# Two groups of matmuls on constants in the first stage of a transformer block

## The chip, the cores and the metric

The kernel runs on one core of a Trainium2 chip. The metric is device time in microseconds of one execution. The core has five engines with queues of their own: PE (TensorE, matrix products and transpositions into the PSUM banks), DVE (VectorE), ACT (ScalarE), POOL (GpSimd) and SP (SyncE, which here issues the DMA transfers). Each works through its instructions in order, and an instruction waits until what it needs from another engine is done.

## The reference

One layer of a trunk with 1024 positions and width 1024, in f32: a token mixer (a short gated convolution beside a stick-breaking attention with 8 heads of 64) and a squared-ReLU MLP. The first stage of the kernel computes the beginning of it: the modulation of the conditioning vector `c`, the normalised and modulated `h`, and the attention's values `v`.

```python
mod = c @ w_ada[l] + b_ada[l]
sh1, sc1, gt1, sh2, sc2, gt2 = jnp.split(mod, N_MOD, axis=-1)

h = modulate(rms_norm(x, g_pre_mix[l]), sh1, sc1)   # h * (1 + sc1) + sh1
proj = h @ w_in[l]
bg, cg, u, q, k, v, ga, gb = jnp.split(proj, split_pts, axis=-1)
y_conv = short_conv_branch(bg, cg, u, conv_w[l]) @ w_proj_conv[l]
o = stick_breaking_attention(q, k, v)               # heads split and joined
merged = jax.nn.sigmoid(ga) * y_conv + jax.nn.sigmoid(gb) * (o @ w_proj_attn[l])
x = x + gt1[:, None, :] * rms_norm(merged @ w_out[l], g_post_mix[l])

h2 = modulate(rms_norm(x, g_pre_mlp[l]), sh2, sc2)
ff = jnp.square(jax.nn.relu(h2 @ w_mlp_in[l])) @ w_mlp_out[l]
x = x + gt2[:, None, :] * rms_norm(ff, g_post_mlp[l])
```

## The kernel before

Products of f32 data are made of three products of split operands: a tensor is split into a rounded part (`hi`, an ACT copy at L104) and the rest (`lo`, a DVE subtraction at L91), and hi x hi, hi x lo and lo x hi are summed in PSUM. The kernel runs through the first stage (modulation, `h` and values), attention with the projections and the convolution, the branches, `w_out`, and the MLP, whose products use a scheme with seven products in place of eight.

The change is in the first stage alone. There positions go in blocks `b` of 128 (0 to 7) and channels in columns `k` of 128 (0 to 7). The stage is written as steps, each a letter and its numbers; a string `order` lists them, and `run` (L524) calls them in turn. `tc.manual_schedule` at L535 keeps the queues of PE and SP in that written order. The orders of ACT, DVE and POOL come from the compiler's planner, which goes by modelled times.

The steps, with the lines at which the profile shows them:

- `x` (`x_block`): loads a block of `x` and normalises it (ACT L403 and L407, or DVE L409; the root on POOL, L132).
- `T` (`turn_all`): transposes all eight columns of a block on PE (L418) into banks with the tag `tr`, of which there are two, and copies them to `xT` (L422). It is used for the blocks 0 to 3.
- `s` (`slab`): loads two columns of `w_ada` for the shift and the scale in four pieces (L440) and sums them, weighted by `c`, on DVE into `acc` (L449 for the first piece, L451 for the others).
- `g` (`gains`): sums `acc` over the partitions with four PE matmuls of one column each (L461). They write four columns of the bank `mod`, which the profile calls `c`. DVE reads two pairs of these columns (L94, into a1 and b1) and finishes a1 (L464). Shifts of `mod` use the columns 0 to 7, scales 8 to 15.
- `w` (`value_rows`): loads rows of `w_in` for the values (L470) and splits them (L104, L91).
- `t` (`turn`): transposes column `k` of one or three blocks into a `tr` bank (L483). Group letters: A is the blocks 0 to 3, B is block 4, C is 5 to 7; a, d, b and c are 0 to 1, 2 to 3, 4, and 5 to 7.
- `h` (`shift`): makes `h` of a column from `xT` or from a `tr` bank, times a1 plus b1, and splits it: ACT L494 with DVE L495, or ACT L498 and L104, then DVE L91 (`hTl`).
- `v` (`values`): three matmuls of 512 columns for each block and column (L508) into one bank per block.

So g02 is the sums of the first slab (columns 0 and 1), va0 the values of blocks 0 and 1 from column 0, tB6 the transposition of column 6 of block 4. The PE queue near the first place holds, in this order, g02, va0, vd0, tB1, tB0, vd1, tB4, vb0, tB2, g22, vb1, va1, tB3; then tB6, vb2, va2, g42, vd2, va3, vb3, vd3, va4, vd4, g62, and after vd5 further on tB5. Each `tr` bank is free again when `shift` has read it.

`ident` and `ones` are constants of 128 x 128 f32 that POOL writes at the start. `mod` is one bank of 512 f32 columns, in use through this stage only.

Of the kernel before, what the change touches and what calls it, by code (L numbers as in the profile page):

```python
# [16 lines left out]
P = 128  # L17
D = 1024
T = 1024
# [7 lines left out]
HALF = 512  # L27
# [3 lines left out]
def block_kernel(  # L31
# [19 lines left out]
    nc = tc.nc  # L51
    x, out = x[0], out[0]
# [28 lines left out]
    def bank(pool, tag, bufs=None):  # L81
        return pool.tile([P, HALF], F32, tag=tag, name=nm(tag), bufs=bufs)
# [267 lines left out]
    ident = cst.tile([P, P], F32, name="ident")  # L350
    make_identity(nc, ident)
    ones = cst.tile([P, P], F32, name="ones")
# [21 lines left out]
    with ExitStack() as es:  # L374
# [15 lines left out]
        mod = bank(pst, "c", 1)  # L390
# [94 lines left out]
        def shift(k, blocks):  # L485
# [6 lines left out]
            hi, lo = hT[0][:, k, to], hT[1][:, k, to]  # L492
            if (k, blocks[0]) in BOTH:
                nc.scalar.activation(hi, src, AF.Identity, scale=ak, bias=bk)  # L494
# [6 lines left out]
        def values(k, blocks):  # L501
            for b in blocks:
# [9 lines left out]
                if k == KC - 1:  # L512
# [2 lines left out]
                        vs[:, b, :, 0, :], vs[:, b, :, 1, :],  # L515
                    )

        BOTH = {(7, 4), (4, 0), (0, 4), (1, 5), (0, 0), (5, 4), (6, 4), (0, 5), (6, 0), (1, 0)}
        NORM_ACT = {2, 3, 4, 7}
        TURN_DVE = {(1, 0), (1, 1), (2, 1)}  # L520
        groups = {"A": (0, 1, 2, 3), "B": (4,), "C": (5, 6, 7), "a": (0, 1), "d": (2, 3), "b": (4,), "c": (5, 6, 7)}
        steps = {"x": x_block, "T": turn_all, "s": slab, "g": gains, "w": value_rows}

        def run(order):  # L524
            for step in order.split():
# [4 lines left out]
                    {"t": turn, "h": shift, "v": values}[what[0]](*n, groups[what[1]])  # L530

        order = """
            x1 x0 x2 T1 x3 s02 T0 T3 T2 g02 hA0 w02 va0 x4 s22 hA1 vd0 tB1 tB0 hB0 w22 vd1 tB4 vb0 hB1 tB2 g22 hB2 vb1 hA2 va1 s42 hA3 tB3 tB6 vb2 va2 hB3 g42 vd2 w42 hA5 va3 vb3 hA4 vd3 s62 x5 va4 hB4 x6 vd4 g62 tB7 vd5 w62 hA6 vb4 va5 x7 hB6 tB5 vd6 va6 hA7 hB5 hB7 vb5 tC0 hC0 tC5 va7 hC5 vb6 tC1 hC1 tC2 vd7 tC3 vc0 hC2 tC4 hC3 tC6 vc1 vc2 tC7 vc3 hC4 vc4 hC6 hC7 vc5 vc6 vb7 vc7
        """
        with tc.manual_schedule(engines={mybir.EngineType.PE, mybir.EngineType.SP}):  # L535
            run(order)
# [723 lines left out]
    steps = [(g, i) for g in range(NG) for i in ORDER]  # L1260
# [236 lines left out]
```

## Time and profile before

| what | us |
|---|---|
| median of three runs | 1435.9 |
| lowest and highest of them | 1434.11, 1441.1 |
| the profiled execution, whole | 1439.44 |
| its span | 1437.7 |

| stretch, us from the start | PE busy | DVE busy | ACT busy | granted clock |
|---|---|---|---|---|
| 0 to 20 | 9.06 | 9.62 | 11.42 | 1.00 |
| 20 to 40 | 12.12 | 18.41 | 11.99 | 0.80 |
| 40 to 60 | 18.66 | 17.36 | 13.55 | 0.94 |
| 60 to 260 | 190.03 | 140.59 | 113.26 | 0.98 |

The first table is device time; the span is the part of the profiled execution in which the engines work. In the second, busy times are sums over the stretch, and the granted clock is PE's, as a share of full speed, averaged over it.

A row of a timeline gives the start, the duration (of several instructions together where a count stands behind), the engine, the line, the operation, output and inputs by name, their shapes, and in brackets how long the engine stood idle before and what ended that. A row of a view of stretches gives the stretch, its length, the busy time of PE, PE's weight loads, DVE, ACT and POOL with their numbers of instructions, the granted clock, the busy share of the DMA engines and GB/s. A row of the view of waits names who waited for whom, the total, how often, and the longest.

### The profile page before, as it was taken

Reading aid. Unit: us, or ns where it says so; the run is one execution under the profiler, and the core shown is the slowest. Engines: PE = TensorE matmul, PEld = TensorE weight load, DVE = VectorE, ACT = ScalarE, POOL = GpSimd, SP = SyncE. Lnnn points to the kernel's source line nnn. Section 1 sums busy time; section 2 is a strip of 40 time slices with the busy share of each in tenths; the row PEclk is TensorE's granted clock in tenths of the full one; section 3 lists DMA queues with packets and bytes.
Section 4 is the critical chain, followed back from the end, with each engine's and each line's share of the span. In section 5 each row is a group of like instructions: output and inputs, shape, how many; then the busy total and the mean of one; then the engine's idle time right before and its main releaser. Section 6 shows DMA issues by size and latency. Waiting matters only on the chain.

```text
span 1437.7 us, 17905 instructions
## 1 busy us (share of the span) xinstructions
PE 1368.7 (95%) x6281; PEld 1120.3 (78%) x6281; DVE 1058.7 (74%) x1656; ACT 653.7 (45%) x1317; POOL 97.2 (7%) x187
## 2 busy tenths in 40 slices
PE   5899899999999999989999899999999999999996
PEld 4788777887888888767878688888888788888884
DVE  6827888887876878637736886555654999898987
ACT  5736656565524444324446634333332554343343
POOL 1003112212200000000001000000000000000002
PEclk9999999999999999999999999999999999999998
DMA  8601110111124776668422243322346452514113
GB/s 296 187 15 39 32 53 22 37 38 52 45 90 141 249 269 199 208 203 319 149 97 100 68 146 117 117 82 95 117 144 221 160 169 83 176 59 154 49 47 117
DMA packets 111741, 178.42 MB, mean 124 GB/s; under 512 B 7786, under 2 KB 67230, under 8 KB 111652
## 3 DMA queue, kind: packets, MB, share of 16 engines
q1 hardware_dynamic: 111652, 177.29, 37.3%
q8 instruction: 49, 0.80, 0.2%
q14 instruction: 40, 0.33, 0.1%
HBM read 135.83 MB, written 41.43 MB: 123 GB/s over the span
## 4 chain that ended last, share of the span: by engine, by line
PE 71%; DVE 14%; DMA 6%; issue 4%; ACT 3%; POOL 1%; SPq 0%; DVEq 0%; ACTq 0%; POOLq 0%
PE s L234 26%; PE s L1371 18%; PE mm L546 10%; PE s L903 3%; PE v L508 3%; DVE pt L690 2%; PE s L122 2%; PE s L123 2%; PE s L121 2%; PE o L731 2%; DMA raw<-in_w_in_dram 2%; DVE a L694 2%; DMA wa<-in_w_ada_dram 2%; PE tr L720 1%; POOL a L686 1%
## 5 line engine op out<-in xcount | busy, mean ns | idle before, releaser
L1371 PE MATMUL s<-y,y 128*128 128x512 f32 x1008 | 239.6, 390 | 0.0
L1371 PEld LDWEIGHTS s<-y,y 128*128 128x128 f32 x1008 | 189.3, 188 | 40.4
L546 PE MATMUL mm<-hTh,wh 128*128 128x512 f32 x320 | 129.1, 403 | 0.0
L546 PE MATMUL mm<-hTh,wl 128*128 128x512 f32 x320 | 125.6, 392 | 0.0
L546 PE MATMUL mm<-hTl,wh 128*128 128x512 f32 x320 | 125.5, 392 | 0.0
L104 ACT CAST y<-g 128x512 fp32r<-128x512 f32 x96 | 53.5, 620 | 114.7 <-PE s L1371 97.0
L690 DVE TENSOR_TENSOR_SCAN pt<-pt,dmask 128x128 f32<-128x128 f32 (+3 forms) x64 | 87.1, 1365 | 8.6 <-ACT pt L683 8.2
L234 PE MATMUL s<-mTh,g 128*128 128x512 f32 x256 | 86.0, 403 | 3.7 <-ACT mTh L104 3.7
L1371 PE MATMUL s<-fr,fr 128*128 128x512 f32 x336 | 87.1, 392 | 1.5 <-DVE fr L91 1.5
L104 ACT CAST tu<-tr 128x512 fp32r<-128x512 f32 (+2 forms) x112 | 49.2, 439 | 78.2 <-PE tr L720 51.6
L132 POOL TENSOR_TENSOR rstd<-var,mhalf 128x1 f32<-128x1 f32 x32 | 25.2, 789 | 871.5 <-DVE var L129 871.4
L91 DVE TENSOR_TENSOR tu<-tr,tu 128x512 fp32r<-128x512 f32 (+2 forms) x112 | 55.1, 494 | 34.5 <-ACT tu L104 33.4
L234 PE MATMUL s<-mTh,h 128*128 128x512 f32 x240 | 79.6, 395 | 0.0
L1381 DVE TENSOR_TENSOR ffacc<-s,ffacc 128x512 f32<-128x512 f32 x96 | 65.5, 691 | 16.9 <-PE s L1371 16.9
L1371 PEld LDWEIGHTS s<-fr,fr 128*128 128x128 f32 x336 | 63.0, 188 | 16.0 <-DVE fr L91 1.9
L234 PE MATMUL s<-y,h 128*128 128x512 f32 x288 | 71.7, 391 | 0.0
L234 PE MATMUL s<-y,g 128*128 128x512 f32 x288 | 71.5, 391 | 0.0
L546 PEld LDWEIGHTS mm<-hTh,wl 128*128 128x128 f32 x320 | 60.2, 188 | 13.4
L234 PE MATMUL s<-hTh,t 128*128 128x512 f32 x208 | 67.6, 394 | 0.0
L546 PEld LDWEIGHTS mm<-hTl,wh 128*128 128x128 f32 x320 | 60.5, 189 | 8.8
L546 PEld LDWEIGHTS mm<-hTh,wh 128*128 128x128 f32 x320 | 60.4, 189 | 8.9
L731 PE MATMUL o<-tu,vs 128*128 128x256 f32 x320 | 56.9, 297 | 9.7 <-DVE ot L741 5.1
(286 smaller groups left out, 3124.0 us busy)
## 6 DMA issues: line engine op xcount, KB each, us to landing
raw<-in_w_in_dram SPq DMA_DIRECT2D x38, 512.0 KB, 5.2
wa<-in_w_ada_dram SPq DMA_DIRECT2D x32, 512.0 KB, 4.0
raw<-in_w_mlp_in_dram SPq DMA_DIRECT2D x32, 512.0 KB, 3.8
f_d<-wl SPq DMA_DIRECT2D x16, 512.0 KB, 4.8
f_d<-wh SPq DMA_DIRECT2D x16, 512.0 KB, 3.2
g<-in_w_mlp_out_dram SPq DMA_DIRECT2D x32, 256.0 KB, 3.7
g<-f_d SPq DMA_DIRECT2D x32, 256.0 KB, 3.2
h<-in_w_mlp_out_dram SPq DMA_DIRECT2D x32, 256.0 KB
```

The costliest lines, as they stand in the source:

```text
L91: eng.tensor_tensor(o, a, b, op=ALU.subtract)
L104: nc.scalar.copy(hi, src)
L121: nc.tensor.matmul(ps, lh, rh, start=i == 0, stop=False)
L122: nc.tensor.matmul(ps, lh, rl, start=False, stop=False)
L234: nc.tensor.matmul(ps, l, r, start=first and k == 0 and j == 0, stop=k == nk - 1 and j == 2, skip_group_check=True,)
L508: nc.tensor.matmul(vb[b], l, r, start=k == 0 and i == 0, stop=k == KC - 1 and i == 2, skip_group_check=True,)
L546: nc.tensor.matmul(ps, w[a][:, k, :], hT[b][:, k, s], start=k == 0 and i == 0, stop=k == KC - 1 and i == 2, skip_group_check=True,)
L690: nc.vector.tensor_tensor_scan(pt[:, 0:w][:, ::-1], pt[:, 0:w][:, ::-1], dmask[:, T - w : T][:, ::-1], 1.0, ALU.mult, ALU.max,)
L731: nc.tensor.matmul(po[:, : 2 * P], v, part[:, 0:5:4, :] if j and jp == g else part[:, 2 * j + 1 : 2 * j + 3, :], start=jp == 0 and j == 0 ...
L903: nc.tensor.matmul(ps, l[:, k, s], r, start=k == 0 and i == 0, stop=k == 3 and i == 2, skip_group_check=True,)
L1371: nc.tensor.matmul(ps, l[:, s], r, start=start and j == 0 and n == 0, stop=stop and j == len(fs) - 1 and n == 2, skip_group_check=True,)
L1381: nc.vector.tensor_tensor(o, ps, o, op=ALU.add)
```

## The change

A step `z` is new. It issues `n` matmuls whose operands are the constants: `ones` is the weights, `ident` the 128 moving columns, both f32. The output goes to the last 128 columns of the bank `mod` (384 to 511), and nothing reads it. The step z8 stands in the order twice: behind g02 (ahead of hA0, so ahead of va0 in PE's queue) and behind tB3, ahead of tB6.

```diff
+        def warm(n):
+
+            for _ in range(n):
+                nc.tensor.matmul(mod[:, HALF - P :], ones, ident, start=True, stop=True)
+
...
-        steps = {"x": x_block, "T": turn_all, "s": slab, "g": gains, "w": value_rows}
+        steps = {"x": x_block, "T": turn_all, "s": slab, "g": gains, "w": value_rows, "z": warm}
...
-            x1 x0 x2 T1 x3 s02 T0 T3 T2 g02 hA0 w02 va0 x4 s22 hA1 vd0 tB1 tB0 hB0 w22 vd1 tB4 vb0 hB1 tB2 g22 hB2 vb1 hA2 va1 s42 hA3 tB3 tB6 vb2 va2 hB3 g42 vd2
+            x1 x0 x2 T1 x3 s02 T0 T3 T2 g02 z8 hA0 w02 va0 x4 s22 hA1 vd0 tB1 tB0 hB0 w22 vd1 tB4 vb0 hB1 tB2 g22 hB2 vb1 hA2 va1 s42 hA3 tB3 z8 tB6 vb2 va2 hB3 g42 vd2
```

The rest of the order is the same in both.

More of the change, by code (lines that the diff above doesn't have):

```diff
@@ L532, in block_kernel @@
         order = """
-            x1 x0 x2 T1 x3 s02 T0 T3 T2 g02 hA0 w02 va0 x4 s22 hA1 vd0 tB1 tB0 hB0 w22 vd1 tB4 vb0 hB1 tB2 g22 hB2 vb1 hA2 va1 s42 hA3 tB3 tB6 vb2 va2 hB3 g42 vd2 w42 hA5 va3 vb3 hA4 vd3 s62 x5 va4 hB4 x6 vd4 g62 tB7 vd5 w62 hA6 vb4 va5 x7 hB6 tB5 vd6 va6 hA7 hB5 hB7 vb5 tC0 hC0 tC5 va7 hC5 vb6 tC1 hC1 tC2 vd7 tC3 vc0 hC2 tC4 hC3 tC6 vc1 vc2 tC7 vc3 hC4 vc4 hC6 hC7 vc5 vc6 vb7 vc7
+            x1 x0 x2 T1 x3 s02 T0 T3 T2 g02 z8 hA0 w02 va0 x4 s22 hA1 vd0 tB1 tB0 hB0 w22 vd1 tB4 vb0 hB1 tB2 g22 hB2 vb1 hA2 va1 s42 hA3 tB3 z8 tB6 vb2 va2 hB3 g42 vd2 w42 hA5 va3 vb3 hA4 vd3 s62 x5 va4 hB4 x6 vd4 g62 tB7 vd5 w62 hA6 vb4 va5 x7 hB6 tB5 vd6 va6 hA7 hB5 hB7 vb5 tC0 hC0 tC5 va7 hC5 vb6 tC1 hC1 tC2 vd7 tC3 vc0 hC2 tC4 hC3 tC6 vc1 vc2 tC7 vc3 hC4 vc4 hC6 hC7 vc5 vc6 vb7 vc7
         """
```

## The prediction

> **What bounds the kernel now.** I read the page first, then PE's waits of the first 85 us, then stretches of 3.4 us, then the timelines of PE, DVE and ACT around the two places.
>
> ```profile
> span 1437.7 us, 17905 instructions
> ...
> PE 1368.7 (95%) x6281; PEld 1120.3 (78%) x6281; DVE 1058.7 (74%) x1656; ACT 653.7 (45%) x1317; POOL 97.2 (7%) x187
> ...
> PE 71%; DVE 14%; DMA 6%; issue 4%; ACT 3%; POOL 1%; SPq 0%; DVEq 0%; ACTq 0%; POOLq 0%
> ```
>
> The kernel as a whole is bound by PE: 1368.7 of 1437.7 us. The first stage is different; there PE waits for others:
>
> ```profile
> PE v L508 <- ACT hTh L494: 3.9, 1, 3.9
> PE tr L483 <- ACT tmp L498: 3.3, 1, 3.3
> ```
>
> The two groups are put into the first two of these waits. What the waits cost beyond themselves is in the granted clock (seventh figure of a row, after the five engines; the first is the length):
>
> ```profile
> 18.50:21.90 3.40, 1.03 (x8) 0.94 (x8) 1.58 (x3) 1.14 (x2) 0.00 (x0) 1.00 0.88 305
> 21.90:25.30 3.40, 1.85 (x4) 1.14 (x5) 3.36 (x11) 2.72 (x6) 0.00 (x0) 0.50 0.88 283
> 25.30:28.70 3.40, 3.40 (x10) 2.62 (x9) 3.33 (x5) 1.18 (x2) 0.98 (x1) 0.50 1.04 367
> 28.70:32.10 3.40, 2.52 (x13) 1.69 (x11) 3.07 (x7) 2.15 (x5) 0.00 (x0) 1.00 1.09 356
> ...
> 35.50:38.90 3.40, 0.50 (x3) 0.14 (x1) 3.23 (x6) 3.40 (x8) 0.00 (x0) 1.00 1.09 352
> 38.90:42.30 3.40, 2.95 (x8) 2.38 (x9) 3.40 (x7) 0.69 (x3) 0.00 (x0) 0.51 1.09 361
> ```
>
> After a stretch in which PE worked 1.03 or 0.50 of 3.40 us the clock is at half in the next; it is full again after one with 3.40 or 2.95, not after 1.85. A stretch with 2.52 (28.70) keeps it. The edges come in steps of 3.4 us, which I take as the clock's own grid. The half-clock time is 6.8 + 3.4 us, and that is all that the change can shorten.
>
> The matmuls of `values` show the price (start, duration, then the row's name):
>
> ```profile
> 26.02 0.63 PE L508 MATMUL v<-wvh,hTl 128*128 128x512 f32 x1
> 26.44 0.63 PE L508 MATMUL v<-wvh,hTh 128*128 128x512 f32 x1
> ...
> 48.22 0.39 PE L508 MATMUL v<-wvl,hTh 128*128 128x512 f32 x1
> 48.44 0.39 PE L508 MATMUL v<-wvh,hTl 128*128 128x512 f32 x1
> ```
>
> They start about 0.43 us apart at half clock and 0.23 apart at full, so 0.20 is lost on each.
>
> **What one group costs.** A call of `warm` multiplies plain f32 constants, 128 columns. No row has that shape. Two have its kind, and a step of `gains` shows that a call becomes two records (four calls, x8):
>
> ```profile
> 32.76 0.95 PE L461 MATMUL c<-ones,acc 128*128 128x1 f32 x8
> ...
> 517.35 0.19 PEld L1012 LDWEIGHTS s<-acc,ones 128*128 128x128 f32 x1 [0.24 <-issue]
> 517.78 0.19 PEld L234 LDWEIGHTS s<-hTh,t 128*128 128x128 f32 x1 [0.24 <-issue]
> ```
>
> With 1 column, eight records take 0.95 us, 0.12 each. With 512 columns on the same `ones`, one takes 0.43, a quarter of which is 0.11. So 0.12 each at full clock, and 16 records take **1.9 us**. Half clock stretches by 0.43/0.23, so 0.225 each and **3.6 us**. The bounds: no less than 16 x 0.12 = 1.9, no more than the half-clock `values` pace, 16 x 0.43 = 6.9, which I don't take because it is that of 512 columns.
>
> **The first group** (z8 behind g02). It writes columns 384 to 511 of `mod`; DVE reads two columns at a time of the same bank behind g02:
>
> ```profile
> 18.48 1.05 PE L461 MATMUL c<-ones,acc 128*128 128x1 f32 x8
> ...
> 22.13 0.15 DVE L94 TENSOR_TENSOR a<-c,vcols 128x2 f32<-128x2 f32 x1
> 22.20 0.15 DVE L94 TENSOR_TENSOR b<-c,vcols 128x2 f32<-128x2 f32 x1
> ...
> 23.45 0.80 PE L508 MATMUL v<-wvh,hTh 128*128 128x512 f32 x1 [3.92 <-ACT hTh L494]
> ...
> 28.89 0.38 PE L483 MATMUL tr<-ident,xb 128*128 128x128 f32 x2
> ```
>
> No row shows whether PE may write other columns of a bank while a reading is outstanding. The start lies between 19.53 (no wait) and 22.35 (both readings done). I take 22.35: where PE waits for a PSUM reader in these rows, as `tr` for ACT tmp L498, it waits for the tile as a whole. The Trainium skill (PSUM — Partial Sum Buffer, "PSUM bank collisions raise a hardware error") says the same: order engines by bank and quadrant, not by address; no run here shows it. That rule speaks against the place of this group: of the 3.92 us of idle time 1.1 are left.
>
> Behind this wait on PE stand twelve matmuls of `values` (va0, vd0) and the transpositions tB1, tB0, for which ACT and then DVE wait. From 22.4 the group runs at half clock: 13 records by 25.3. The stretch 21.9 to 25.3 then has 2.9 us of work, as the one that ended at 42.30 with 2.95 and a raised clock. If the clock rises at 25.3, the other 3 records end at 25.7, twelve matmuls at 0.23 end at **28.4 against 28.89**: half a microsecond early. Without a rise, records end at 26.0, six matmuls by 28.7 and the other six at 30.0: 1.1 late. The first is my forecast, barely.
>
> Little of that half microsecond gets through, since DVE bounds this part. It worked 3.07 to 3.40 of 3.40 us in each stretch above from 21.90 on, and from 28.9 to 43.07 it shows one wait, 0.20:
>
> ```profile
> 29.80 0.41 DVE L495 TENSOR_SCALAR tmp<-tr,a,b 128x128 f32<-128x128 f32 x1 [0.20 <-ACT hTh L494]
> 30.30 0.69 DVE L91 TENSOR_TENSOR wvl<-raw,wvh 128x512 fp32r<-128x512 f32 x1
> ...
> 43.95 0.16 DVE L94 TENSOR_TENSOR a<-c,vcols 128x2 f32<-128x2 f32 x1 [0.88 <-PE c L461]
> ...
> 52.37 0.16 DVE L94 TENSOR_TENSOR a<-c,vcols 128x2 f32<-128x2 f32 x1 [0.83 <-PE c L461]
> ```
>
> That gap and the 0.09 between the first row's end (30.21) and the second's start can go: **-0.3 us**. Lateness would go through in full.
>
> **The second group** (z8 ahead of tB6).
>
> ```profile
> 33.82 0.15 DVE L94 TENSOR_TENSOR b<-c,vcols 128x2 f32<-128x2 f32 x1
> ...
> 35.73 0.27 PE L483 MATMUL tr<-ident,xb 128*128 128x128 f32 x1
> ```
>
> DVE's last reading of `mod` ends at 33.97, so nothing holds the group; PE is free at 36.0 with a full clock. The group ends at 37.9, ahead of tB6, whose bank comes free at 39.35 whatever PE does (bounded by 0.23 x 16 = 3.7 it would end at 39.7, 0.4 late). The stretch 35.50 to 38.90 then has 2.4 us of work in place of 0.50. That lies between 1.85, which didn't raise the clock, and 2.52, which kept it; this row has less and kept it too, the next stretches being full:
>
> ```profile
> 56.00:59.40 3.40, 2.11 (x10) 1.76 (x11) 2.51 (x7) 3.04 (x5) 0.65 (x2) 1.00 0.88 249
> 60.00:80.00 20.00, 20.00 (x101) 16.66 (x100) 8.09 (x16) 9.56 (x18) 2.00 (x3) 1.00 0.01 4
> ```
>
> So the clock stays. The Trainium skill (TensorE: Matmul & The Clock Gate, "HAM oscillation — how this bites in real kernels") puts the drop at idle gaps over about 3.4 us; by that rule alone a gap of 3.35 us needs no filling, and this group would save nothing. The row of 0.50 us of work, followed by half clock, already goes against so literal a reading.
>
> Now the gain, step by step:
>
> ```profile
> 39.35 0.48 PE L483 MATMUL tr<-ident,xb 128*128 128x128 f32 x1 [3.35 <-ACT tmp L498]
> ...
> 42.97 0.95 PE L461 MATMUL c<-ones,acc 128*128 128x1 f32 x8
> ...
> 51.39 0.95 PE L461 MATMUL c<-ones,acc 128*128 128x1 f32 x8
> ...
> 57.29 0.33 PE L483 MATMUL tr<-ident,xb 128*128 128x128 f32 x1 [1.34 <-DVE tmp L495]
> ```
>
> From tB6 to g42 PE takes 3.62 us for one transposition and nine matmuls. At full clock these need 0.13 + 9 x 0.23 = 2.2, so g42 comes 1.4 early, 1.7 with the 0.3 above. DVE, free at 43.07 - 0.3, then finds its sums and loses its wait of 0.88 (-1.2 in all); PE runs on to g62, 1.7 early if its operands keep up (DVE, which makes them, is 1.2 early as well), which also takes DVE's wait of 0.83 away. tB5 at 57.29 waits for DVE, so DVE's gain counts, not PE's: -1.7 by 52.37. Between them lies one fixed point:
>
> ```profile
> 52.52 1.05 ACT L104 CAST wh<-raw 128x1024 fp32r<-128x1024 f32 x1 [0.54 <-issue]
> ...
> 53.89 2.35 DVE L91 TENSOR_TENSOR wl<-raw,wh 128x1024 fp32r<-128x1024 f32 x2
> ```
>
> The second half of that DVE row can't start before ACT ends at 53.57 if ACT waits there for a transfer; it started at 55.07, so 1.5 at most can pass. With that, and a tenth for the rounding, **1.4 us** of the 1.7 arrive at tB5; behind it PE is busy for all of 60 to 80 us, so it is passed on. SP's queue is unchanged in order; `warm` issues no transfers, adds nothing to DVE or ACT, and its 32 records of PE stand in idle time except for the 2.3 us of the first group counted above.
>
> **Sum.** -0.3 (first group) - 1.4 (second) + 0.3 (lost at the fixed point and in rounding) = -1.4 us. The profiled execution took 1439.44 (span 1437.7 and 1.7 around it), so it would become 1438.0. The median shown is 1435.9, 3.5 below the profiled one: **1434.5**.
>
> **The rivals.**
> 1. **The first group doesn't wait for DVE.** It runs from 19.5 and is done by 23.1 even at 3.6 us; the clock is full at 23.45 and the matmuls end by 26.9. DVE still gives only its 0.3, so -1.7 by DVE's count and -1.5 behind the fixed point: 1434.4. For it: the columns are disjoint. Against: the waits above are by tile. 0.15.
> 2. **Slower: the groups don't count as work for the clock.** For it speak the first transpositions, which are f32 with 128 columns and the constant `ident` as well:
>
> ```profile
> L418 PE MATMUL tr<-ident,wh x16: 417/421/476, 9.1 to 16.2; 128*128 128x128 f32 x16
> ...
> L483 PE MATMUL tr<-ident,xb x32: 270/272/476, 28.9 to 73.1; 128*128 128x128 f32 x32
> ```
>
>    From 9.1 to 18.4 they fill most of PE's time and yet all last 421 ns, against 270 later on (the clock's column, 1.00 there, has no sign of it). Were `warm` like them, the clock would rise at 28.7 as before: the first group pushes tB1 and tB0 by 1.1, DVE carries that on, and the second group holds nothing: +1.1, 1437.0. Against it: `warm` makes ordinary matmuls. It decides as soon as the group that starts at 22.4 misses the rise at 25.3. The Trainium skill (TensorE: Matmul & The Clock Gate, "Part 4: PE-mode transpose") says of transpositions that they don't engage the full clock, which agrees with the 421 ns; of this kind of matmul it says nothing. 0.20.
> 3. **Nothing gets through**: the transfer at 52.5 or the later waits take it all, 1435.9. For it: PE isn't the only bound of the next stage, where it worked 190 of 200 us. 0.10.
>
> ```profile
> 60.00:260.00 200.00, 190.03 (x982) 158.69 (x981) 140.59 (x200) 113.26 (x244) 35.39 (x78) 0.98 0.11 32
> ```
>
> 4. **The orders of DVE and ACT change.** They are no part of the diff but are planned by the compiler from modelled times that now contain 32 more records. PE idles 1437.7 - 1368.7 = 69 us in all; a tenth or so of it, 8 us, could come or go: 1428 or 1444. 0.15, evenly by sign.
>
> **Numbers.** The forecast has 0.40. Faster or slower by over 0.5% (7.2 us, about what a measurement can tell) needs case 4 with most of its price: 0.05 each, and 0.90 stays within. The three runs before lie between 1434.11 and 1441.1, so a median moves by itself by 2 or 3 us. The range takes in cases 1 to 3, that spread, and part of case 4: 1428.5 to 1441.
>
> **What would show it.** Right: in the profile after, sixteen records of the first group start behind DVE's L94 at about 22.4; the clock is full before 26 and doesn't drop at 38.9; the nine matmuls behind tB6 start 0.23 apart; DVE's waits for `c` at 43.95 and 52.37 are gone; tB5 starts near 55.9. Wrong: the first group starts before 20 (case 1); `values` starts 0.43 apart until 28.7, and behind tB6 (case 2); the order of DVE's or ACT's rows differs (case 4); or the wait ahead of tB5 grows by what PE gained (case 3).

## The result and the profile after

The changed kernel takes 1444.09 us (median of 19 runs, 1438.15 to 1448.37) against 1437.08 us (19 runs, 1433.85 to 1441.2) of the kernel before on the same chip: ratio 1.0039, 95% interval 1.0029 to 1.005. It is slower by 5.6 us by the ratio and by 7.0 us by the medians, which is within 0.5% but on the other side of the forecast, and above the range that was given.

The head of the page of the changed kernel:

```profile
span 1443.3 us, 17967 instructions
...
PE 1373.6 (95%) x6313; PEld 1124.5 (78%) x6313; DVE 1059.1 (73%) x1656; ACT 651.8 (45%) x1317; POOL 96.3 (7%) x187
```

PE has its 32 records more, 6313 in place of 6281. The work of the other engines is the same in number. The view of PE's waits up to 85 us:

```profile
PE c L521 <- DVE b L94: 3.3, 1, 3.3
PE v L508 <- DVE hTl L91: 2.5, 2, 1.7
```

The two longest waits of before that were shown (3.9 for ACT hTh, 3.3 for ACT tmp) are gone, as meant. In their place the first group itself waits for DVE's reading of the bank, and `values` waits longer for a `hTl`. Now PE's timeline of the changed kernel, at the places that the prediction names:

```profile
22.97 3.78 PE L521 MATMUL c<-ident,ones 128*128 128x128 f32 x16 [3.33 <-DVE b L94]
...
33.98 0.64 PE L508 MATMUL v<-wvh,hTl 128*128 128x512 f32 x1 [1.75 <-DVE hTl L91]
...
40.38 2.26 PE L521 MATMUL c<-ident,ones 128*128 128x128 f32 x16
42.48 0.27 PE L483 MATMUL tr<-ident,xb 128*128 128x128 f32 x1
...
44.67 0.95 PE L461 MATMUL c<-ones,acc 128*128 128x1 f32 x8
...
53.11 0.94 PE L461 MATMUL c<-ones,acc 128*128 128x1 f32 x8
...
59.75 0.33 PE L483 MATMUL tr<-ident,xb 128*128 128x128 f32 x1 [1.06 <-DVE tmp L495]
...
86.59 0.39 PE L551 MATMUL mm<-hTh,wh 128*128 128x512 f32 x1
```

The last row is the first product of the projections, so it marks the end of the first stage. Against before, g42 is 1.70 us later (42.97 to 44.67), g62 1.72 (51.39 to 53.11), tB5 2.46 (57.29 to 59.75). The stage ends 2.5 us later; the row of before is

```profile
84.08 0.39 PE L546 MATMUL mm<-hTh,wh 128*128 128x512 f32 x1
```

So nearly half of the 5.6 us between the spans of the two profiles (1437.7 and 1443.3) is lost ahead of the first product, and this part grows at two places: by 40 us, and between g62 and tB5. Stretches of the changed kernel for the first place (clock in the seventh figure):

```profile
25.30:28.70 3.40, 3.40 (x15) 3.00 (x15) 3.33 (x7) 1.74 (x2) 0.98 (x1) 0.70 1.08 363
...
32.10:35.50 3.40, 1.65 (x8) 1.36 (x8) 3.33 (x9) 0.00 (x0) 0.00 (x0) 0.81 1.08 362
35.50:38.90 3.40, 3.40 (x11) 2.82 (x12) 2.95 (x8) 1.98 (x4) 0.00 (x0) 0.50 1.09 352
```

A new hole stands at 32 to 34 us, with PE at 1.65 of 3.40, and after it the clock is at half again, for work that ran at full clock before. The row at 33.98 waits for a `hTl`, and DVE shows why that is late:

```profile
30.19 0.69 DVE L91 TENSOR_TENSOR wvl<-raw,wvh 128x512 fp32r<-128x512 f32 x1
...
31.46 0.69 DVE L91 TENSOR_TENSOR wvl<-raw,wvh 128x512 fp32r<-128x512 f32 x1
...
32.46 0.40 DVE L495 TENSOR_SCALAR tmp<-tr,a,b 128x128 f32<-128x128 f32 x1
...
33.64 0.28 DVE L91 TENSOR_TENSOR hTl<-tmp,hTh 128x128 fp32r<-128x128 f32 x1
```

Both splits `wvl<-raw` now stand ahead of DVE's piece of hB0, `tmp<-tr`. Before, that piece came at 29.80, ahead of both (the row is in the prediction). ACT's rows changed as well. First two rows of the kernel before, then six of the changed one:

```profile
34.80 0.46 ACT L498 ACTIVATE tmp<-tr,b,a 128x128 f32<-128x128 f32 x1 [3.31 <-DVE a L464]
...
37.28 1.14 ACT L104 CAST wvh<-raw 128x512 fp32r<-128x512 f32 x2
```

```profile
29.54 1.15 ACT L104 CAST wvh<-raw 128x512 fp32r<-128x512 f32 x2 [1.41 <-DMA raw<-in_w_in_dram]
30.58 0.45 ACT L494 ACTIVATE hTh<-tr,b,a 128x128 fp32r<-128x128 f32 x1
...
36.92 1.14 ACT L104 CAST wvh<-raw 128x512 fp32r<-128x512 f32 x2 [5.20 <-DMA raw<-in_w_in_dram]
37.96 0.45 ACT L498 ACTIVATE tmp<-tr,b,a 128x128 f32<-128x128 f32 x1
...
40.96 0.46 ACT L498 ACTIVATE tmp<-tr,b,a 128x128 f32<-128x128 f32 x1
...
56.86 0.82 ACT L494 ACTIVATE hTh<-xT,b,a 128x512 fp32r<-128x512 f32 x1 [2.24 <-DVE a L464]
```

The casts `wvh<-raw` are split work of `value_rows`, the others are `shift`. In the changed kernel both pairs of casts stand ahead of the pieces of `h`, and wait for their transfer with the pieces behind them: `tmp` comes at 37.96, not at 34.80. PE, held up by the hole and by half clock, comes to tB3 only at 40.17. So the bank that tB6 needs comes free at 41.42 (the `tmp` at 40.96 and its 0.46), not at 39.35. The second group, which was to end ahead of that, holds PE until 42.48, so 1.06 us of it stand in tB6's way. **The order of ACT's instructions has changed, and so has DVE's.** The second place is DVE's alone:

```profile
54.07 1.22 DVE L91 TENSOR_TENSOR wl<-raw,wh 128x1024 fp32r<-128x1024 f32 x1
55.20 0.15 DVE L94 TENSOR_TENSOR a<-c,vcols 128x2 f32<-128x2 f32 x1
...
55.34 1.21 DVE L91 TENSOR_TENSOR wl<-raw,wh 128x1024 fp32r<-128x1024 f32 x1
...
56.67 0.15 DVE L464 SCALAR_TENSOR_TENSOR a<-a,vcols 128x2 f32<-128x2 f32 x1
```

g62's product is there at 54.05 (53.11 + 0.94). Before, DVE took it up as soon as it came (the row at 52.37 in the prediction, with a wait of 0.83) and split `wl`, an operand of the next stage, behind it. Now half of `wl` stands ahead of the readings and the other half ahead of L464, which finishes a1. The last row comes 2.6 us after the product, and ACT waits 2.24 for it (at 56.86 above).

The two programs confirm it: the same instructions of DVE and ACT, in another order in the first stage, and again in the first product of the MLP, where PE's order differs too. The change touches neither. The planner works out these orders from modelled times, and 32 PE records tip them.

### The profile page after: what moved, and what is told of

The parts are those of the page before. It is cut to its first block, busy times and chain, and to the rows that moved or that the text cites. A ratio compares the mean times of both kernels' runs of the same rounds, so it can differ in the third digit from the quotient of the medians.

```text
span 1443.3 us, 17967 instructions
## 1 busy us (share of the span) xinstructions
PE 1373.6 (95%) x6313; PEld 1124.5 (78%) x6313; DVE 1059.1 (73%) x1656; ACT 651.8 (45%) x1317; POOL 96.3 (7%) x187
## 4 chain that ended last, share of the span: by engine, by line
PE 69%; DVE 14%; DMA 8%; issue 4%; ACT 3%; POOL 1%; SPq 1%; DVEq 0%; ACTq 0%; POOLq 0%
PE s L234 23%; PE s L1376 18%; PE mm L551 10%; PE s L908 3%; DMA wa<-in_w_ada_dram 3%; PE s L123 3%; PE s L121 3%; PE s L122 3%; DVE pt L695 2%; PE o L736 2%; PE v L508 2%; DVE a L699 2%; DMA raw<-in_w_in_dram 2%; PE tr L725 1%; DVE acc L145 1%
## 5 line engine op out<-in xcount | busy, mean ns | idle before, releaser
L1376 PE MATMUL s<-y,y 128*128 128x512 f32 x1008 | 239.7, 390 | 0.0
L1376 PEld LDWEIGHTS s<-y,y 128*128 128x128 f32 x1008 | 189.2, 188 | 40.4
L551 PE MATMUL mm<-hTh,wh 128*128 128x512 f32 x320 | 129.1, 403 | 0.0
L551 PE MATMUL mm<-hTh,wl 128*128 128x512 f32 x320 | 125.6, 392 | 0.0
L551 PE MATMUL mm<-hTl,wh 128*128 128x512 f32 x320 | 125.5, 392 | 0.0
L1376 PE MATMUL s<-fr,fr 128*128 128x512 f32 x336 | 88.5, 396 | 2.6 <-DVE fr L91 2.6
L91 DVE TENSOR_TENSOR tu<-tr,tu 128x512 fp32r<-128x512 f32 (+2 forms) x112 | 55.0, 493 | 34.7 <-ACT tu L104 33.8
L1376 PEld LDWEIGHTS s<-fr,fr 128*128 128x128 f32 x336 | 64.0, 191 | 17.6 <-DVE fr L91 3.1
L551 PEld LDWEIGHTS mm<-hTh,wl 128*128 128x128 f32 x320 | 60.2, 188 | 13.4
L551 PEld LDWEIGHTS mm<-hTl,wh 128*128 128x128 f32 x320 | 60.5, 189 | 8.9
L551 PEld LDWEIGHTS mm<-hTh,wh 128*128 128x128 f32 x320 | 60.4, 189 | 8.8
```

Source lines behind the costliest of these rows:

```text
L91: eng.tensor_tensor(o, a, b, op=ALU.subtract)
L551: nc.tensor.matmul(ps, w[a][:, k, :], hT[b][:, k, s], start=k == 0 and i == 0, stop=k == KC - 1 and i == 2, skip_group_check=True,)
L1376: nc.tensor.matmul(ps, l[:, s], r, start=start and j == 0 and n == 0, stop=stop and j == len(fs) - 1 and n == 2, skip_group_check=True,)
```

## The experiments

The kernels of each table ran on one chip, with runs of the kernel before beside them. The questions: do the groups cost, or the orders; which part of the orders; and do the two add up?

**The groups in smaller portions.** The edit is in the order string; with no call or six in the first group the planner keeps the orders of the kernel before, with seven it takes the changed kernel's.

```diff
-... g02 hA0 w02 ... hA3 tB3 tB6 ...
+second_only:      ... g02 hA0 w02 ... hA3 tB3 z8 tB6 ...
+six_and_eight:    ... g02 z6 hA0 w02 ... hA3 tB3 z8 tB6 ...
+seven_and_eight:  ... g02 z7 hA0 w02 ... hA3 tB3 z8 tB6 ...
```

> The second group alone (z8 ahead of tB6), without the first. The planned orders of DVE, ACT, POOL and SP and the later part of PE's are those of before, instruction by instruction. Theory O (the loss of the change, 5 to 6 us, comes from the orders that the planner changed in the first stage and in the MLP's first product): 1 to 1.5 us faster than before, or no different, since no order moves; the clock stays full at 38.9 and tB5 starts about 1 us earlier. Theory W (the loss comes from the first group itself, which waits for DVE and pushes the values): the same for this run. Theory G (both groups cost PE time that nothing hides): 1 to 3 us slower.

> Both groups, the first with six matmuls in place of eight. All planned orders are those of before. Theory O: within 2 us of before (the first group still waits for DVE's readings and pushes the values by 1 to 2 us, the second gives 1.4 back), so 3 us or more faster than the changed kernel. Theory W: 3 to 6 us slower than before, as the changed kernel, less half a microsecond for the two matmuls left out.

> Both groups, the first with seven matmuls. All planned orders are those of the changed kernel. It has one matmul call (two records, 0.2 to 0.5 us) more than the run with six. Theory O: 4 to 6 us slower than before, and at least 3 slower than the run with six. Theory W: no more than 1 us slower than the run with six.

| kernel | median, us | ratio | 95% interval | first stage ends |
|---|---|---|---|---|
| before, same chip | 1437.43 | | | 84.1 |
| second_only | 1437.43 | 1.0005 | 0.9991 to 1.0018 | 83.8 |
| six_and_eight | 1438.68 | 1.0014 | 1.0 to 1.0029 | 83.2 |
| seven_and_eight | 1441.76 | 1.0033 | 1.0019 to 1.0048 | 86.0 |

(The stage's end is the start of the first L546 or L551 row in each kernel's one profile; that of before is the profile shown above.) From six to seven calls, one matmul more, the median goes up by 3.1 us and the stage ends 2.8 us later. The seventh call itself adds 0.42 us to the first group, which takes 3.35 us in place of 2.93.

The second group alone does what was forecast to the clock. PE's timeline of second_only, and a stretch:

```profile
39.56 0.33 PE L483 MATMUL tr<-ident,xb 128*128 128x128 f32 x1 [1.54 <-ACT tmp L498]
41.80 0.94 PE L461 MATMUL c<-ones,acc 128*128 128x1 f32 x8
...
56.70 0.33 PE L483 MATMUL tr<-ident,xb 128*128 128x128 f32 x1 [1.89 <-DVE tmp L495]
```

```profile
38.90:42.30 3.40, 2.74 (x16) 2.36 (x16) 3.40 (x6) 0.90 (x3) 0.00 (x0) 1.00 1.10 360
```

The clock doesn't drop at 38.9 (0.51 in this stretch before), tB6 to g42 takes 2.24 us in place of 3.62, and g42 is 1.17 early. But tB5 is only 0.59 early and the stage's end 0.2: the wait ahead of tB5 grew from 1.34 to 1.89. That is rival 3, in part. It is one execution, though, and one without a group can have g42 as early; late_order_only, below, shows it.

**The orders apart from the groups.** late_order_only has no groups but two calls `z2` ahead of the stage's last step; it gets the changed kernel's order in the MLP's first product and keeps that of before in the first stage. In the other kernels DVE, ACT and where needed PE are held to a given order by a chain of dependencies between neighbours of the same engine, of the kind `NoSync`, which is to fix the order and nothing else:

```diff
-            ... vb7 vc7
+            ... vb7 z2 vc7
```

```diff
+    def issue_in(engine, count, order):
...
+        for p, q in zip(order, order[1:]):
+            tc.add_manual_dep(
+                mine[q], mine[p].name,
+                mybir.DependencyInfo(mybir.DependencyClass.NoSync, mybir.DependencyReason.DATA),
+                reason="issue order",
+            )
...
+    issue_in(mybir.EngineType.DVE, 1656, DVE_ORDER)
+    issue_in(mybir.EngineType.Activation, 1251, ACT_ORDER)
```

> Neither group; two matmul calls on constants (0.5 us) at the end of the first stage, ahead of its last three products. The first stage's orders are those of before, the orders of PE, DVE, ACT and SP in the MLP's first product are those of the changed kernel. It splits theory O: if the later orders carry half of the loss, 2.5 to 3.5 us slower than before; if the first stage's orders carry all that isn't chance, 0.5 us slower. Theory W: 0.5 us slower.

Measured: 1437.66, ratio 1.0011 (0.9998 to 1.0024), the stage ends at 83.3. By its median the order in the MLP costs nothing. The interval allows 3.4 us, but groups_first_new, below, has the whole loss without that order.

groups_old_order has both groups and the orders of before; first_order_no_groups has no group and the changed kernel's first-stage orders; all_orders_no_groups has no group and all of the changed kernel's orders.

> The whole change, both groups of eight, but DVE and ACT are held to the order of before by edges between instructions of one engine (order alone, no waits); PE, POOL and SP are as before but for the groups. Theory O (the order of the first stage makes the loss): 0 to 2.5 us slower than before, as the run with six and eight. Theory W (the first group's own wait and its eight matmuls make it): 4 to 6 us slower, as the changed kernel.

> No groups at all; DVE and ACT are held to the changed kernel's order in the first stage, and everything behind it to the order of before. Theory O: 2 to 4 us slower than before, without any matmul on constants. Theory W: no different from before (within 1 us). A third reading, B (the new order costs only together with the groups, because it is fit to a late tB1): 1 us slower at most.

> No groups; the orders of the changed kernel on all engines, in the first stage and in the MLP's first product. Theory O: 2.5 to 5 us slower than before, that is the run with the first stage's order plus 0 to 1.5 us for the later orders (the run with the late order alone gave 0 to 1.5 beyond its half microsecond of work). Theory W and reading B: within 1.5 us of before.

| kernel | median, us | ratio | 95% interval | first stage ends |
|---|---|---|---|---|
| before, same chip | 1437.48 | | | |
| groups_old_order | 1437.28 | 0.9998 | 0.9984 to 1.0012 | 83.4 |
| first_order_no_groups | 1439.25 | 1.0013 | 0.9999 to 1.0027 | 88.1 |
| all_orders_no_groups | 1438.84 | 1.0004 | 0.9992 to 1.0016 | 87.0 |

The late end of the first stage goes with the orders and not with the groups. But the time of the whole kernel goes up by less than the stage loses: an untidy result, taken up below.

**A first group that needn't wait.** early_four_and_eight writes its first group of four calls into the bank of `v` for block 0, which nobody reads then, so that it can start at once; orders as before.

```diff
+        def early(n):
+            vb[0] = bank(pst, "v", 5)
+            for _ in range(n):
+                nc.tensor.matmul(vb[0][:, HALF - P :], ones, ident, start=True, stop=True)
...
-                if not k:
+                if not k and b not in vb:
...
+            ... g02 y4 hA0 ... tB3 z8 tB6 ...
```

> The first group has four matmuls and writes into the bank that the first values will fill, which no reader holds, so it starts at 19.6 without waiting for DVE; the second group is as in the change. All orders are those of before. If the wait for DVE is what keeps the first group from helping, the clock is at full speed when the values start (23.4), the twelve matmuls end by 27, and the time is 1 to 3 us under before; if DVE and the transfers bound the stage whatever the clock does, it is within 1.5 us of before.

Measured: 1438.68, ratio 1.0003 (0.9989 to 1.0017). Its PE timeline, and a stretch:

```profile
20.28 2.05 PE L527 MATMUL v<-ident,ones 128*128 128x128 f32 x8
...
26.50 0.63 PE L508 MATMUL v<-wvh,hTl 128*128 128x512 f32 x1
26.93 0.63 PE L508 MATMUL v<-wvh,hTh 128*128 128x512 f32 x1
...
27.77 0.40 PE L508 MATMUL v<-wvh,hTl 128*128 128x512 f32 x1
```

```profile
25.30:28.70 3.40, 3.40 (x10) 2.61 (x11) 3.33 (x7) 1.65 (x2) 0.98 (x1) 1.00 1.06 366
```

The group runs in the hole without a wait. But the clock was not full, whatever the column says. Eight records took 2.05 us, where 16 take 3.78 at half clock and 1.95 at full, and the products of `values` start 0.43 apart up to 27.35 and 0.23 apart from 27.77. The clock's column stands at 1.00 from the start of this profile, and the rise at 27.7 doesn't show in it. So the condition of this experiment, a full clock when the values start, didn't come about, and it doesn't say what that is worth.

late_order_only says it by chance. Up to its two calls at 80.78 its program is that of before, but its clock rose at 26.5, not at 28.7. A stretch of it, three rows of PE and one of DVE:

```profile
25.30:28.70 3.40, 3.40 (x14) 2.70 (x14) 3.33 (x5) 1.61 (x2) 0.97 (x1) 0.83 1.08 369
```

```profile
27.80 0.38 PE L483 MATMUL tr<-ident,xb 128*128 128x128 f32 x2
...
32.19 0.95 PE L461 MATMUL c<-ones,acc 128*128 128x1 f32 x8
...
41.02 0.95 PE L461 MATMUL c<-ones,acc 128*128 128x1 f32 x8
```

```profile
29.42 0.41 DVE L495 TENSOR_SCALAR tmp<-tr,a,b 128x128 f32<-128x128 f32 x1
```

tB1 comes 1.09 us early (28.89 before), DVE's piece behind it 0.38 (29.80), g22 0.57 (32.76). DVE works 3.33 of 3.40 us in this stretch, and about half of what PE gains gets through. g42 comes 1.95 early (42.97), more than with the second group in second_only, and no group stands ahead of it.

**Which part of the new orders, with the groups.** groups_first_new has both groups, the changed kernel's orders in the first stage, and before's in the rest; groups_front_new takes only the front part of the first-stage orders (with ACT's early casts), groups_rear_new only the rear part (with `wl` ahead of g62's readings); change_again is the changed kernel itself. The edit is in the lists given to `issue_in`. Each was run five or six times only.

> Both groups of eight, the changed kernel's order of DVE and ACT in the first stage, the order of before behind it. Theory O: 2.5 to 4 us slower than before, with tB5 at 59 to 60 and the projections from 86 to 87, and 0 to 1.5 us faster than the changed kernel. If it is as slow as the changed kernel (5 us), the MLP's order has no share; if it is within 1 us of before, the MLP's order carries the loss together with the groups.

> Both groups, the changed kernel's order only in the front part: on DVE up to the last sum of the fourth slab, on ACT up to the squares of x5 (about 47 us); behind that the order of before. If the front part carries the loss (the pieces of hB0 behind two splits, the splits of w42 ahead of three pieces of h): 1.5 to 2.5 us slower, the projections start at 85 to 86. If the rear part does: no different from the groups in the old order, 83.4.

> Both groups, the changed kernel's order only in the rear part (the normalising of x5 and x6 and the first projection's split ahead of a1 and b1 from g62). If this part carries the loss: 0.7 to 1.5 us slower, the wait ahead of tB5 longer by 0.7 than in the old order. If the front does: no different from the groups in the old order.

> The changed kernel as it is, on the chip of these three. Theory O: 4 to 6 us slower than before, at least 3 more than the groups in the old order gave, and as much as front, rear and MLP order together.

| kernel | median, us | ratio | 95% interval | first stage ends |
|---|---|---|---|---|
| before, same chip | 1436.28 | | | |
| groups_first_new | 1442.46 | 1.0036 | 1.0023 to 1.005 | 86.2 |
| groups_front_new | 1443.44 | 1.0046 | 1.0032 to 1.0061 | 84.7 |
| groups_rear_new | 1441.3 | 1.0033 | 1.002 to 1.0046 | 84.3 |
| change_again | 1442.07 | 1.0038 | 1.0025 to 1.0052 | 86.6 |

The orders of the first stage, with the groups, are enough for the whole loss (groups_first_new). But each half of them seems enough too, although their first stage ends only 0.2 to 0.6 us late. Either groups and orders together cost more than their sum, or the chips differ.

**The square.** Groups alone, orders alone, both, and the rear half once more, on one chip. The kernels are groups_old_order, all_orders_no_groups, the changed kernel and groups_rear_new.

> Both groups, DVE and ACT held to the order of the kernel before; timed a second time so that it stands on one chip beside the orders alone and the whole change. Theory A (the orders alone cost, the groups nothing): 0.9998 as the first time, within 0.9985 to 1.001. Theory B (the groups cost only together with the new orders): the same here. Theory C (the first comparison was of two chips, and on this one the groups cost as well): 1.002 or more.

> No group; DVE, ACT and PE held to the changed kernel's orders; a second time, beside the whole change. A: as much as the whole change, 1.003 to 1.0045. B: 1.0000 to 1.0015, as the first time, with the first stage still 2 to 4 us late in its profile. C: depends on the chip, anything between.

> The changed kernel itself, beside its two halves on one chip. A, B: 1.0035 to 1.0045. If it comes out under 1.002 here, its cost depends on the chip (C), and all the comparisons between calls have to be read with that in mind.

> Both groups, and of the changed kernel's first-stage orders only the rear part. In its first run the first stage ended 0.2 us later than before, and the time was 4.7 us longer. A: under 1.001, since its first stage ends no later. B: 1.0025 to 1.0045 again. C: follows the other three.

| kernel | median, us | ratio | 95% interval | first stage ends |
|---|---|---|---|---|
| before, same chip | 1437.41 | | | |
| square_groups | 1438.69 | 1.0007 | 0.9994 to 1.002 | 83.4 |
| square_orders | 1440.14 | 1.0021 | 1.0007 to 1.0035 | 86.5 |
| square_change | 1443.02 | 1.0041 | 1.0027 to 1.0056 | 86.8 |
| square_rear | 1439.82 | 1.0017 | 1.0001 to 1.0033 | 85.3 |

On this chip the orders without any group are slower than the kernel before, by 2.7 us of the medians, and the groups without the orders aren't measurably so. The changed kernel keeps its loss on every chip; theory C, that it is a matter of the chip, falls for it. For theory A the orders alone cost too little, for theory B too much: 1.0007 and 1.0021 add up to 1.0028, and 1.0041 is 1.9 us above that, about as much as the interval of one ratio is wide to one side. So the square excludes neither a plain sum nor one of these two theories. groups_rear_new came out at 1.0033 first and at 1.0017 here, with intervals that overlap, so its first number isn't to be leaned on.

What the orders do in the first stage is beyond doubt, since square_orders shows the changed kernel's waits without a single `warm`. ACT's and PE's timelines:

```profile
36.78 1.14 ACT L104 CAST wvh<-raw 128x512 fp32r<-128x512 f32 x2 [5.20 <-DMA raw<-in_w_in_dram]
...
56.72 0.82 ACT L494 ACTIVATE hTh<-xT,b,a 128x512 fp32r<-128x512 f32 x1 [2.23 <-DVE a L464]
```

```profile
59.61 0.33 PE L483 MATMUL tr<-ident,xb 128*128 128x128 f32 x1 [1.06 <-DVE tmp L495]
...
86.45 0.39 PE L546 MATMUL mm<-hTh,wh 128*128 128x512 f32 x1
```

The same 5.20 and 2.2 us, tB5 at 59.61 and the stage's end at 86.45 (59.75 and 86.59 in the changed kernel). And square_groups, with every `warm` and the orders of before:

```profile
22.99 3.78 PE L521 MATMUL c<-ident,ones 128*128 128x128 f32 x16 [3.31 <-DVE b L94]
...
29.58 0.38 PE L483 MATMUL tr<-ident,xb 128*128 128x128 f32 x2
...
40.04 0.33 PE L483 MATMUL tr<-ident,xb 128*128 128x128 f32 x1 [1.56 <-ACT tmp L498]
...
42.27 0.95 PE L461 MATMUL c<-ones,acc 128*128 128x1 f32 x8
...
56.61 0.33 PE L483 MATMUL tr<-ident,xb 128*128 128x128 f32 x1 [1.35 <-DVE tmp L495]
```

Here tB1 is 0.69 late behind the first group, g42 0.70 early behind the second, tB5 0.68 early. Over all profiles the stage ends at 83.2 to 84.1 us in the seven with before's orders in it, and at 86.0 to 88.1 in the eight with all of the changed kernel's.

**What stays open.** Orders alone, three measurements: 1.0004, 1.0013, 1.0021, or 0.6 to 3.0 us. Groups alone, two: 0.9998 and 1.0007, and 1.0014 with six calls in the first group. Both together, with all first-stage orders new: 1.0033 to 1.0041 in five. By the means (1.0037 against 1.0013 and 1.0003) some 3 us seem to appear only when both are there; they are taken from several chips, and on the one chip of the square it is 1.9 us, within the noise. Part of this may lie at the other end of the kernel. In the last stage PE waits 2.6 us for a `fr` of DVE in the changed kernel (L1376 for L91) and 1.7 in square_groups. Behind the longer wait the clock drops, and the stage with its 1008 products `s<-y,y` lasts 315.1 us in place of 312.7. DVE is late there because it waited for a transfer, 4.2 us for `f_d<-wl` in the changed kernel and 3.5 in square_groups. Of the eight profiles with groups and new orders five show a wait of 2.5 or more and 314 to 315 us, of the ten others one (early_four_and_eight). On average the stage lasts 314.2 us in these eight and 312.0 in the three with the orders alone, while the first stage ends no later in the eight. These are single executions, and no run separated the cause, so it isn't claimed. Nor was a version found that beats the kernel before.

## Why the prediction was wrong

**The step that failed** is in the part on the second group: "`warm` issues no transfers, adds nothing to DVE or ACT". It adds no instruction to them, but it changed their order, and the sum of -1.4 us took those orders as given. The prediction had this as its fourth rival, with 0.15 and no sign; it was the case that came, at +5.6 us (7.0 by the medians), inside the 8 us that were put on it. The chance was too small. The prediction knew that the orders are planned from modelled times; with 32 new records in a stage where DVE has no slack, unchanged orders needed a reason, and none was given. The range reached into this case only to +5 us and ended 3.1 us below the median. 1.2 us of the miss are the start: it took 1435.9 for the kernel before, from three runs, and 19 give 1437.08.

**With the orders held**, the -1.4 us wasn't seen either: 0.9998 and 1.0007, -0.2 and +1.3 us of the medians. The first interval still allows it (0.9984 is -2.3 us), the second no longer (0.9994 is -0.9). In the first stage the groups show no gain beyond the spread of single executions: it ends at 83.2 to 83.9 us in the five profiles with groups and before's orders, and at 84.1 and 83.3 in the two without a group there (before and late_order_only). Point by point:

- The first group waits for DVE's readings of the other columns of its bank: right. It was to start at 22.35; it starts at 22.99 in square_groups and 22.97 in the changed kernel, with the wait named for `b` L94. Rival 1 is out.
- Sixteen records at half clock in 3.6 us: 3.78. At full clock 1.9: 1.95 where a group ran at full clock throughout. Right.
- "If the clock rises at 25.3": wrong. A mean clock of 0.70 over 25.3 to 28.7 in the changed kernel means full clock for the last 1.4 us, so it rose at 27.3; in square_groups tB1 came 0.69 late, not half a microsecond early. In change_again the clock rose at 25.8 and tB1 came 0.21 early (28.68), so either branch can come. The prediction took the edges of the clock's grid from the profile of before, as if they belonged to the program. They don't: see below. Which branch a profile shows is luck.
- DVE hides part of what PE gains by the faster clock there: right. The forecast let 0.3 us of half a microsecond through; in late_order_only 0.57 of 1.09 reached g22. early_four_and_eight, built to show it, ran at half clock there.
- The second group ends ahead of tB6's bank and keeps the clock: right in second_only and square_groups, wrong in the changed kernel, where it ends 1.06 us behind. 3.62 us from tB6 to g42 became 2.23 in square_groups (40.04 to 42.27), where 2.2 was forecast. Of these 1.39 us g42 kept 0.70, because tB6 came 0.69 late behind the first group.
- 1.4 us arrive at tB5: mis-sized. 0.68 came with both groups and 0.59 with the second alone, where the wait ahead of tB5 took back half. At the stage's end that is 0.2 to 0.6 us, which a ratio with an interval of 1.9 us to each side can't show.
- Rival 2, that `warm` doesn't count as work for the clock: out. In change_again the first group by itself raised it (see below).

What made the forecast look safe was that each of its terms was small and its sign argued for. But the one thing that the edit could move outside PE was larger than all of them.

## What to carry to other kernels

Where a planner orders some engines by modelled times, an edit on another engine is an edit to their order too: compare the instruction order of every engine before looking at any time, and pin the orders to test the edit itself. A stall on an engine is worth filling only if the engine behind it has slack; here 0.57 of the 1.09 us that a faster clock gave PE arrived, because DVE was at 3.33 of 3.40. A clock that a profile shows has to be checked by the spacing of equal rows before a conclusion is drawn from it; early_four_and_eight shows why. And look among the rows behind a short, urgent instruction (here a1 and b1) for long ones that a planner may put ahead of it, such as the split of an operand that the next stage needs.

## What the runs showed of the hardware

**The clock's grid is not tied to the program.** A stretch of the changed kernel:

```profile
18.50:21.90 3.40, 1.05 (x8) 0.97 (x8) 1.05 (x3) 1.06 (x2) 0.00 (x0) 0.80 0.87 297
```

A mean of 0.80 puts the drop at 20.5 us; in the kernel before it comes at 21.9 (the prediction's rows: 1.00 up to there, 0.50 behind). The way back differs too: before and late_order_only run the same program up to 80 us, and the clock rises at 28.7 in the one and at 26.5 in the other, which alone moves tB1 by about 1 us. So what a filler gains there isn't one number, and a profile of one execution doesn't give it. The Trainium skill (TensorE: Matmul & The Clock Gate, "What's actually happening") says that the window runs freely and doesn't start with the kernel; these runs agree.

**Products of constants count as work for the clock.** change_again has nothing else on PE between 20 and 25.79 us:

```profile
22.38 3.68 PE L521 MATMUL c<-ident,ones 128*128 128x128 f32 x16 [2.54 <-DVE b L94]
```

```profile
25.30:28.70 3.40, 3.40 (x17) 2.84 (x17) 3.13 (x5) 1.16 (x1) 0.55 (x1) 0.92 1.01 349
```

Sixteen records in 3.68 us are half clock. The mean of 0.92 from 25.3 on puts the rise at 25.8, where the group ends and `values` begins.

**Transpositions do raise the clock.** In the changed kernel PE does nothing but these from 9.3 to 17 us:

```profile
11.40 1.97 PE L418 MATMUL tr<-ident,wl 128*128 128x128 f32 x8
14.80 1.14 PE L418 MATMUL tr<-ident,wh 128*128 128x128 f32 x8 [1.43 <-ACT wh L407]
```

Eight took 1.97 us, and the next eight, of the same shape, 1.14. In the profile of before all four eights took 1.97. The row of 421 ns on which the prediction's second rival rested was half clock, which the clock's column doesn't show ahead of its first change (the 1.00 for 0 to 20 us in the table of stretches before is such a value). The Trainium skill (TensorE: Matmul & The Clock Gate, "Part 4: PE-mode transpose") says that the full clock doesn't engage for PE's transpose mode; for the f32 transpositions of this kernel the trace shows otherwise.
